# Differential-attention heads with two buffer sets and the order q, k, v; at the SwiGLU's seam half a row scaling on ScalarE and one token sum on GpSimd

## The chip, the cores and the metric

The kernel runs on one core of a Trainium2 chip. The metric is the device time of one execution in microseconds (us). Times of several runs are given as their median; a profile is one further execution, with a time of its own.

## What is computed

One layer of a streaming encoder block over 512 tokens of width 1024, with 16 meta tokens put ahead of them (528 rows in all), everything in float32:

```
xn   = rmsnorm(h)
proj = xn @ w_in                      # stick-breaking q|k|v, differential q|k|v; 8 heads each
o_sb = stick_breaking_attention(sq, sk, sv)          # strictly causal, no softmax
p    = softmax(dq @ dk + alibi bias, masked)         # two maps per head, c = 0, 1
o_df = rmsnorm((p[0] - lam * p[1]) @ dv) * (1 - lam_init)
gates  = sigmoid(xn @ w_gate + b_gate)
merged = gates[0] * (o_sb @ w_br_sb) + gates[1] * (o_df @ w_br_df)
h = h + merged @ w_out
h = h + (silu(hn @ w_ffn_gate) * (hn @ w_ffn_up)) @ w_ffn_down      # hn = rmsnorm(h)
y = rmsnorm(h), meta rows dropped
```

A stick-breaking head has 128 columns. A differential head has two maps of 64 columns for q and k, and 128 columns for v.

## The kernel before, in words

**Arithmetic.** Every float32 matrix product is made of three products of a rounded high part and a remainder: high times high, high times low, low times high (`mm3`, L224; its three matmuls stand at L227, L228 and L229 wherever it is called). So every operand has to be split: a cast on ScalarE (L75) and a subtraction on VectorE (L76).

**Weights.** They are read from HBM once, in 512 KB pieces, in the order of the list `stream` (L86 to L117). A piece lands in one of three staging tiles `wst` (issued from SyncE's queue, L144), is split into `wh` and `wl` (four buffers each), and is then used. `weights(key)` (L215) also has the next pieces split: three ahead before the first differential piece, two ahead after it (L221).

**Stages by time.** 0 to 40 us: norm and transposes of x. Then eight stick-breaking heads, up to about 260 us; eight differential heads, up to about 510; the gates and the merge (540 to 593); `merged @ w_out` (to 640); the SwiGLU's gate and up products; its down product; the final norm.

**One head.** While head h computes its scores and maps, TensorE is also given units of other work: the projections of head h+1 (two units each for q, k and v), the transposition of head h+1's v (`turn`), and two units of a branch projection `y` of earlier heads. The generator `df_head` (L622) yields numbers, and the loop at L948 runs so many units at each yield. In the differential heads the units stand in the order v, q, k (L618), then the first y unit, `turn`, the second y unit. So between the scores of the token tiles 0, 1, 2 and 3 lie v, v and the first half of q; after the last scores come the rest of q and the two halves of k; then `t1` (transposes of the attention weights), a y unit, `t2` (the rest of these transposes), `turn` and the second y unit, and then `av` (attention weights times v).

**Program order and issue order.** The head loop is not in a hand-written order: the framework's scheduler orders the instructions of each engine by priority among those that it holds ready, so that an engine can be given a later unit where an earlier one would wait. [...] The framework also puts in every wait, and it hands out the buffers of a tag in a ring: a new tile waits until the tile that had the buffer has been read for the last time.

**q and k of a differential head.** Each map c has a tile `dq`, 128 x 512: rows of one half hold the high part, rows of the other half the remainder; and a tile `dk`, 128 x 2 x 528. ScalarE and VectorE write one half of `dk`'s partitions (L611, L612), and a DMA from GpSimd's queue copies this half to the other partitions (L615). There is one buffer of each, so that the next head's q can only be written when the present head's scores have been made. The scores are made at L632 and L633.

**PSUM.** Eight banks: `z`, two tiles of two banks each, for scores, for the transposes of the attention weights (L493, L507, L510, in the function `attn_out`, L482), and for `av`; and `mm`, four tiles of one bank (`mm_tile`, `tr_tile`), for projections, y units, `turn` and the heads' norm. In `attn_out`, `turn_first` makes the transposes of blocks 0 and 1 into the two banks of one `z` tile, and `turn_rest` makes block 2 and the small blocks into another. Each block is read by ScalarE (L495) and then by VectorE (L496).

**y.** A y tile of 128 x 512 is copied out of PSUM by ScalarE (L725) into a buffer, from which a DMA on GpSimd's queue writes it to DRAM, or adds it there (L727, L729). The buffers are, in turn, one of two `ys` and one of two `sg0` tiles; for the last two y pieces four tiles named w0 to w3.

**The tag y_sb in the pool xtp.** One buffer of 16 KB a partition. The tile `tA` (token sums for the stick-breaking heads, L272) has it first, and then `hres` (L997), into which the residual input x is loaded in four DMAs of 512 KB (L999, GpSimd's queue). `hres` is first read at L1031.

**The tag y_df in opool.** One buffer too: `xs` (the input), then `tB` (more token sums for the stick-breaking heads), then `hn` (L1054).

**The seam.** Between `merged @ w_out` and the SwiGLU stand the row norm (`normed`, L1057: the row's reciprocal root r, then `hn = hres * r` on VectorE, 128 x 1024, once for each of four token tiles), the transposes (`turned`, L1061), and sums and differences of blocks of the transposed tokens (`block_sums`, L1080), from which the SwiGLU's seven-product form takes its operands t1 to t4. TensorE's first products with t2 wait on L1089, VectorE's remainder of t2.

Of the kernel before, what the change touches and what calls it, by code (L numbers as in the profile page):

```python
# [9 lines left out]
F32 = mybir.dt.float32  # L10
F32R = mybir.dt.float32r
# [5 lines left out]
P = 128  # L17
# [23 lines left out]
def block_kernel(ctx: ExitStack, tc: tile.TileContext, x, meta, norm_mix_g, w_in, w_gate, b_gate,  # L41
# [50 lines left out]
    for h in range(NH):  # L92
        for i in (2, 0, 1):
            cols(("df", h, i), w_in, (3 + i) * D + h * P)
        if h < 3:
            rows(("y_sb", h + 5), w_br_sb, (h + 1) % 2 * 512, (h + 5) // 2 * 2)
        else:
            rows(("y_df", h - 3), w_br_df, (h + 1) % 2 * 512, (h - 3) // 2 * 2)
# [116 lines left out]
    def weights(key):  # L215
        at = at_of[key]
        if at < START:
            return loaded[key]
        if at >= first_ffn:
            return fpools["down"](key)  # L220
        prepare(prep_at[key] + (READY if at < at_of["df", 0, 2] else 2))  # L221
        return loaded[key]
# [46 lines left out]
    ydram = ctx.enter_context(tc.tile_pool(name="ydram", bufs=1, space=bass.MemoryType.DRAM))  # L269
    y_count = [0]  # L270

# [209 lines left out]

    def attn_out(blocks, d, lo_rows):  # L482

# [14 lines left out]
        def turn_first():  # L498
            z = z_tile()
            turn(0, z[:, 0])  # L500
            turn(1, z[:, 1])

        def turn_rest():
            z = z_tile()
            turn(2, z[:, 0])
            pt = z[:, 1]
            nc.tensor.transpose(pt[:, 384:512], blocks(3, 3 * P, 4 * P), ident)  # L507
# [42 lines left out]
    def sb_head(h, d, o_h, o_l):  # L550
# [31 lines left out]
        base = ((0, 0), (0, 144), (0, 416), (1, 0))  # L582
        t1, t2, av = attn_out(lambda t, k0, k1: res[base[t][0]][:, base[t][1] + k0:base[t][1] + k1], d, 96)
        yield 4 if h + 1 < SEVEN else 5
# [9 lines left out]
    def df_units(h):  # L594
        d = {}
        hs = (slice(0, 64), slice(64, 128))
        q = [ap_.tile([P, SEQ], F32R, tag=("qh", "ql")[c], name=f"dq{c}") for c in range(2)]
        k = [ap_.tile([P, 2, L], F32R, tag=("kh", "kl")[c], name=f"dk{c}") for c in range(2)]
        d["q"], d["k"] = q, k
# [17 lines left out]
        kv, turn = kv_all("df", h, k_evac, d)  # L617
        return d, kv[2:4] + halves(("df", h, 0), xT, QT, q_evac) + kv[0:2], turn  # L618

    late = []  # L620

    def df_head(h, d, o_h, o_l):  # L622
# [55 lines left out]
        maps(3)  # L678
        t1, t2, av = attn_out(lambda t, k0, k1: prs[t][:, 0, k0:k1], d, 64)
        yield 3 if h < NH - 1 else 2  # L680
        t1()
        yield 1
        t2()
        yield 2
        ps = av()
# [23 lines left out]
    def y_units(name, i, o):  # L709

        def unit(fs):
            wh, wl = weights((name, i))
            for f in fs:
                ps = mm_tile()
                cs = slice(f % 4 * P, (f % 4 + 1) * P)
                mm3(ps, [(wh[:, k, cs], wl[:, k, cs], o[0][:, k], o[1][:, k]) for k in range(2)])

                if name == "y_df" and i > 5:
                    ys = ap_.tile([P, SEQ], F32, tag=f"w{y_count[0] % 4}", name="ys")
                elif y_count[0] % 2:  # L720
# [200 lines left out]
    for br in range(2):  # L921
        name, head = (("y_sb", sb_head), ("y_df", df_head))[br]
        if br:
            nc.gpsimd.memset(a_s, 0.0)
        for h in range(NH):
            if (br, h) == (0, 0):
# [130 lines left out]
    def normed(t):  # L1057
        r = rstd(ssq[t][:, 1:2], more=ssq[t][:, 0:1])()
        nc.vector.tensor_scalar(hn[:, t], hres[:, t], r, None, op0=ALU.mult)

# [19 lines left out]
    def block_sums():  # L1080
# [3 lines left out]
        split(*tsum["t1"], b11)  # L1084
        nc.vector.tensor_tensor(b12, b22, b12, op=sub)
        nc.vector.tensor_tensor(b22, b11, b22, op=add)
        th, tl = tsum["t2"]
        nc.scalar.activation(th, b22, AF.Copy, scale=-1.0)
        nc.vector.scalar_tensor_tensor(tl, b22, -1.0, th.bitcast(F32), op0=ALU.mult, op1=sub)  # L1089
        nc.vector.tensor_tensor(b21, b22, b21, op=sub)  # L1090
        for n, v in (("t3", b12), ("t4", b21)):
# [199 lines left out]
```

## Time and profile before

| what | value |
|---|---|
| time, three runs | 997.58, 999.05, 1001.49 us; median 999.05 us |
| the profiled execution: its own time | 1000.49 us |
| the profiled execution: span from the first to the last instruction | 998.6 us |
| mean granted TensorE clock | 0.993 |
| TensorE matmuls, busy | 970.5 us (97%) |
| VectorE, busy | 687.9 us (69%) |
| ScalarE, busy | 572.2 us (57%) |
| GpSimd, busy | 158.2 us (16%) |
| moved by DMA | 114.12 MB, mean 114 GB/s |

All times below count from the start of the span. PE is TensorE's matmul, PEld its weight load, DVE VectorE, ACT ScalarE, POOL GpSimd, SP SyncE; an L and a number name a line of the kernel. A row of the timeline has the start, the length, the engine, the line, the operation, the tiles written and read, the shapes and the count; in square brackets how long the engine had been idle and what ended this. A row of the list of waits says who waited for whom: the total, the number of times and the longest. A row of a table by stretches has, for each engine, its busy time and in brackets the number of its instructions; then the granted TensorE clock, the busy share of the DMA engines and the GB/s. [...]

### The profile page before, as it was taken

How to read it: one execution, taken by the hardware profiler on the slowest of the kernel's cores; microseconds unless marked ns; L12 is line 12 of the kernel's file. 1: busy time of each engine (PE TensorE's matmuls, PEld its weight loads, DVE VectorE, ACT ScalarE, POOL GpSimd, SP SyncE). 2: the span in 40 equal slices, each digit the busy share in tenths (PEclk: the TensorE clock that was granted, in tenths of full speed). 3: DMA queues.
4: the chain of work that ended last, by engine and by line, in shares of the span. 5: the costliest groups of instructions: out<-in, count | busy, mean ns of one | idle time of the engine just before them, and what ended most of it. 6: DMA issues, size and time to landing. Idle time of an engine off the chain costs nothing.

```text
span 998.6 us, 16211 instructions
## 1 busy us (share of the span) xinstructions
PE 970.5 (97%) x6213; PEld 870.4 (87%) x6213; DVE 687.9 (69%) x1244; ACT 572.2 (57%) x1091; POOL 158.2 (16%) x216
## 2 busy tenths in 40 slices
PE   7999999989999999999999999989999999999996
PEld 5998888879888998889878888879999999988885
DVE  8998678764567777678632633798888888754544
ACT  5676766665566666666772533575555555643533
POOL 4010112121232222322314530000000000000103
PEclk9999999998999999999999999999999999999999
DMA  7312444465563444643838732223343434332212
GB/s 214 86 43 65 127 131 96 97 190 127 127 142 105 93 129 128 148 109 92 161 84 209 223 117 85 85 78 114 94 118 94 119 90 122 100 112 99 92 43 85
DMA packets 140241, 114.12 MB, mean 114 GB/s; under 512 B 4962, under 2 KB 115715, under 8 KB 140163
## 3 DMA queue, kind: packets, MB, share of 16 engines
q1 hardware_dynamic: 129810, 89.29, 29.7%
q0 software_dynamic: 10192, 23.73, 11.9%
q8 instruction: 49, 0.80, 0.3%
q14 instruction: 30, 0.24, 0.1%
q10 hardware_dynamic: 160, 0.07, 0.0%
HBM read 89.87 MB, written 18.87 MB: 109 GB/s over the span
## 4 chain that ended last, share of the span: by engine, by line
PE 78%; DVE 8%; ACT 6%; DMA 5%; issue 2%; POOL 1%; SPq 0%; DVEq 0%; POOLq 0%; ACTq 0%
PE mm L229 18%; PE mm L227 18%; PE mm L228 18%; PE z L227 6%; PE z L229 6%; PE z L228 6%; DMA dk<-dk 3%; PE z L493 1%; ACT wh L75 1%; PE z L632 1%; DVE wl L76 1%; PE z L633 1%; DMA wst<-in_w_in_dram 1%; DVE s L578 1%; DMA xs<-in_x_dram 1%
## 5 line engine op out<-in xcount | busy, mean ns | idle before, releaser
L76 DVE TENSOR_TENSOR wl<-wst,wh 128x1024 fp32r<-128x1024 f32 (+1 forms) x150 | 170.0, 1137 | 118.9 <-ACT wh L75 118.7
L228 PE MATMUL mm<-xT_l,wh 128*128 128x264 f32 (+2 forms) x656 | 213.7, 326 | 2.2 <-DVE xT_l L828 2.2
L227 PE MATMUL mm<-xT_h,wh 128*128 128x264 f32 (+2 forms) x656 | 214.6, 327 | 0.6 <-ACT xT_h L827 0.6
L229 PE MATMUL mm<-xT_h,wl 128*128 128x264 f32 (+2 forms) x656 | 213.5, 325 | 0.0
L75 ACT CAST wh<-wst 128x1024 fp32r<-128x1024 f32 (+1 forms) x150 | 145.8, 972 | 98.9 <-PE mm L228 40.4
L228 PEld LDWEIGHTS mm<-xT_l,wh 128*128 128x128 f32 x656 | 124.2, 189 | 11.6 <-DVE xT_l L828 2.4
L227 PEld LDWEIGHTS mm<-xT_h,wh 128*128 128x128 f32 x656 | 124.4, 190 | 10.3 <-ACT xT_h L827 1.1
L229 PEld LDWEIGHTS mm<-xT_h,wl 128*128 128x128 f32 x656 | 124.1, 189 | 9.8
L228 PE MATMUL mm<-hT_l,wh 128*128 128x256 f32 x284 | 80.5, 284 | 0.7 <-DVE hT_l L1074 0.7
L227 PE MATMUL mm<-hT_h,wh 128*128 128x256 f32 x284 | 80.2, 284 | 0.6 <-DVE sg L1169 0.6
L229 PE MATMUL mm<-hT_h,wl 128*128 128x256 f32 x284 | 80.1, 283 | 0.0
L660 ACT ACTIVATE pr<-pr,nm 128x144 f32<-128x144 f32 (+3 forms) x64 | 36.3, 568 | 40.4 <-DVE nm L658 40.4
L228 PEld LDWEIGHTS mm<-hT_l,wh 128*128 128x128 f32 x284 | 53.7, 189 | 1.2 <-DVE hT_l L1074 1.1
L227 PEld LDWEIGHTS mm<-hT_h,wh 128*128 128x128 f32 x284 | 53.4, 189 | 1.1 <-DVE sg L1169 0.7
L229 PEld LDWEIGHTS mm<-hT_h,wl 128*128 128x128 f32 x284 | 53.6, 189 | 0.0
L227 PE MATMUL mm<-o_h,wh 128*128 128x512 f32 x128 | 52.3, 410 | 0.3 <-ACT o_h L703 0.3
L229 PE MATMUL mm<-o_h,wl 128*128 128x512 f32 x128 | 51.6, 404 | 0.0
L228 PE MATMUL mm<-o_l,wh 128*128 128x512 f32 x128 | 50.0, 392 | 0.0
L227 PE MATMUL mm<-t_h,wh 128*128 128x256 f32 x168 | 47.4, 282 | 1.3 <-ACT wh L75 1.0
L228 PE MATMUL mm<-t_l,wh 128*128 128x256 f32 x168 | 47.3, 281 | 1.1 <-DVE t_l L1089 1.1
L475 POOL COPY v_s<-vT 128x16 f32<-128x16 f32 x64 | 17.8, 307 | 190.6 <-ACT vT L480 82.3
L229 PE MATMUL mm<-t_h,wl 128*128 128x256 f32 x168 | 47.3, 281 | 0.0
(314 smaller groups left out, 2508.0 us busy)
## 6 DMA issues: line engine op xcount, KB each, us to landing
wst<-in_w_in_dram SPq DMA_DIRECT2D x40, 512.0 KB, 4.1
wst<-in_w_ffn_gate_dram SPq DMA_DIRECT2D x22, 512.0 KB, 3.7
wst<-in_w_ffn_down_dram SPq DMA_DIRECT2D x22, 512.0 KB, 3.5
wsu<-in_w_ffn_up_dram SPq DMA_DIRECT2D x21, 512.0 KB, 3.8
wst<-in_w_gate_dram SPq DMA_DIRECT2D x16, 512.0 KB, 4.6
y_df<-ys POOLq DMA_DIRECT2D x20, 256.0 KB, 6.2
dk<-dk POOLq DMA_DIRECT2D x16, 264.0 KB, 5.8
wst<-in_w_br_sb_dram SPq DMA_DIRECT2D x8, 512.0 KB, 4.9
```

Of the source, the lines that this page charges most:

```text
L75: (hi_copy or nc.scalar.copy)(hi, src)
L76: (lo_eng or nc.vector).tensor_tensor(lo, src, hi.bitcast(F32), op=ALU.subtract)
L227: nc.tensor.matmul(ps, lhsT=ah, rhs=bh, start=(start and i == 0), stop=False, skip_group_check=skip)
L228: nc.tensor.matmul(ps, lhsT=ah, rhs=bl, start=False, stop=False, skip_group_check=skip)
L229: nc.tensor.matmul(ps, lhsT=al, rhs=bh, start=False, stop=(stop and i == n - 1), skip_group_check=skip)
L475: nc.gpsimd.tensor_copy(v_s[:, 32 * t:32 * t + NM], vT[:, (t + 1) * P:(t + 1) * P + NM])
L493: nc.tensor.transpose(pt[:, (t - j) * P:(t - j + 1) * P], blocks(t, j * P, (j + 1) * P), ident)
L578: nc.vector.tensor_tensor_scan(f, f, f, 0.0, op0=ALU.add, op1=ALU.bypass)
L632: nc.tensor.matmul(o, lhsT=q[c][:, qs], rhs=k[c][:, 0, k0:k1], start=True, stop=False)
L633: nc.tensor.matmul(o, lhsT=q[c][:, qs], rhs=k[c][:, 1, k0:k1], start=False, stop=True)
L660: nc.scalar.activation(pr[:, c], pr[:, c], AF.Exp, bias=nm[:, c:c + 1], accum_out=ls[:, t, c:c + 1])
```

## The change

1. The pieces of a differential head are streamed and projected in the order q, k, v instead of v, q, k; the look-ahead of weights changes at the first differential piece as before, which is now q.
2. Differential heads with an odd number have their q and k in a second set of buffers: one tile `dqk` in opool's tag `y_df`. Heads with an even number keep the old buffers.
3. In differential heads the transposes of the attention weights go to four `mm` tiles of one bank each instead of two `z` tiles. Stick-breaking heads keep `z`.
4. After `t2` one unit is run ahead of `av` instead of two.
5. From the start of the differential branch on, the y copies go in turn to the eight slots of one new tile `y_out`. It takes the tag `y_sb` in xtp, between `tA` and `hres`.
6. At the seam, `hn` is made in two halves, columns 0 to 511 on VectorE and 512 to 1023 on ScalarE.
7. In `block_sums` the difference `b12 = b22 - b12` (128 x 1024) moves from VectorE to GpSimd, and the sum behind it is written to `b11` instead of `b22`, so that it needn't wait for that difference.

```diff
     for h in range(NH):
-        for i in (2, 0, 1):
+        for i in range(3):
             cols(("df", h, i), w_in, (3 + i) * D + h * P)
...
-        prepare(prep_at[key] + (READY if at < at_of["df", 0, 2] else 2))
+        prepare(prep_at[key] + (READY if at < at_of["df", 0, 0] else 2))
...
-    y_count = [0]
+    y_count, y_out = [0], []
...
-    def attn_out(blocks, d, lo_rows):
+    def attn_out(blocks, d, lo_rows, banks):
...
         def turn_first():
-            z = z_tile()
-            turn(0, z[:, 0])
-            turn(1, z[:, 1])
+            for j, pt in enumerate(banks()):
+                turn(j, pt)
 
         def turn_rest():
-            z = z_tile()
-            turn(2, z[:, 0])
-            pt = z[:, 1]
+            p2, pt = banks()
+            turn(2, p2)
...
     # sb_head
-        t1, t2, av = attn_out(lambda t, k0, k1: ..., d, 96)
+        t1, t2, av = attn_out(lambda t, k0, k1: ..., d, 96,
+                              lambda: (lambda z: (z[:, 0], z[:, 1]))(z_tile()))
...
     def df_units(h):
-        q = [ap_.tile([P, SEQ], F32R, tag=("qh", "ql")[c], name=f"dq{c}") for c in range(2)]
-        k = [ap_.tile([P, 2, L], F32R, tag=("kh", "kl")[c], name=f"dk{c}") for c in range(2)]
+        if h % 2:
+            both = opool.tile([P, 4 * L + 2 * SEQ], F32R, tag="y_df", name="dqk", bufs=1)
+            q = [both[:, 4 * L + c * SEQ:4 * L + (c + 1) * SEQ] for c in range(2)]
+            k = [both[:, 2 * c * L:2 * (c + 1) * L].rearrange("p (a l) -> p a l", a=2) for c in range(2)]
+        else:
+            q = [ap_.tile([P, SEQ], F32R, tag=("qh", "ql")[c], name=f"dq{c}") for c in range(2)]
+            k = [ap_.tile([P, 2, L], F32R, tag=("kh", "kl")[c], name=f"dk{c}") for c in range(2)]
...
-        return d, kv[2:4] + halves(("df", h, 0), xT, QT, q_evac) + kv[0:2], turn
+        return d, halves(("df", h, 0), xT, QT, q_evac) + kv, turn
...
     # df_head
-        t1, t2, av = attn_out(lambda t, k0, k1: prs[t][:, 0, k0:k1], d, 64)
+        t1, t2, av = attn_out(lambda t, k0, k1: prs[t][:, 0, k0:k1], d, 64, lambda: (tr_tile(), tr_tile()))
         yield 3 if h < NH - 1 else 2
         t1()
         yield 1
         t2()
-        yield 2
+        yield 1
         ps = av()
...
     # y_units
-                if name == "y_df" and i > 5:
-                    ys = ap_.tile([P, SEQ], F32, tag=f"w{y_count[0] % 4}", name="ys")
+                if y_out:
+                    ys = y_out[0][:, y_count[0] % KT]
                 elif y_count[0] % 2:
...
         if br:
             nc.gpsimd.memset(a_s, 0.0)
+            y_out.append(xtp.tile([P, KT, SEQ], F32, tag="y_sb", name="y_out"))
...
     def normed(t):
-        nc.vector.tensor_scalar(hn[:, t], hres[:, t], r, None, op0=ALU.mult)
+        nc.vector.tensor_scalar(hn[:, t, 0:512], hres[:, t, 0:512], r, None, op0=ALU.mult)
+        nc.scalar.activation(hn[:, t, 512:D], hres[:, t, 512:D], AF.Copy, scale=r)
...
     # block_sums
-        nc.vector.tensor_tensor(b12, b22, b12, op=sub)
-        nc.vector.tensor_tensor(b22, b11, b22, op=add)
+        nc.gpsimd.tensor_tensor(b12, b22, b12, op=sub)
+        nc.vector.tensor_tensor(b11, b11, b22, op=add)
         th, tl = tsum["t2"]
-        nc.scalar.activation(th, b22, AF.Copy, scale=-1.0)
-        nc.vector.scalar_tensor_tensor(tl, b22, -1.0, th.bitcast(F32), op0=ALU.mult, op1=sub)
-        nc.vector.tensor_tensor(b21, b22, b21, op=sub)
+        nc.scalar.activation(th, b11, AF.Copy, scale=-1.0)
+        nc.vector.scalar_tensor_tensor(tl, b11, -1.0, th.bitcast(F32), op0=ALU.mult, op1=sub)
+        nc.vector.tensor_tensor(b21, b11, b21, op=sub)
```

More of the change, by code (lines that the diff above doesn't have):

```diff
@@ L582, in sb_head @@
         base = ((0, 0), (0, 144), (0, 416), (1, 0))
-        t1, t2, av = attn_out(lambda t, k0, k1: res[base[t][0]][:, base[t][1] + k0:base[t][1] + k1], d, 96)
+        t1, t2, av = attn_out(lambda t, k0, k1: res[base[t][0]][:, base[t][1] + k0:base[t][1] + k1], d, 96,
+                              lambda: (lambda z: (z[:, 0], z[:, 1]))(z_tile()))
         yield 4 if h + 1 < SEVEN else 5
```

## The prediction

> **What bounds the kernel now.** I read the page, then the list of waits of TensorE, then a table by stretches, and at each stretch where TensorE was short of work the timelines of the engines.
>
> ```profile
> span 998.6 us, 16211 instructions
> PE 970.5 (97%) x6213; PEld 870.4 (87%) x6213; DVE 687.9 (69%) x1244; ACT 572.2 (57%) x1091; POOL 158.2 (16%) x216
> ```
>
> TensorE is the bound, nearly everywhere. So an edit can gain only where TensorE waits or runs slowly, and no more than that: about 28 us of 998.6 over the whole span, of which the first 40 us (the start) are not touched. The waits of TensorE over the whole span, the ones that the change can reach:
>
> ```profile
> PE z L507 <- DVE a_l L496: 2.7, 1, 2.7
> PE z L632 <- DMA dk<-dk: 2.2, 6, 0.6
> PE tr L476 <- POOL v_s L475: 1.3, 2, 1.0
> PE mm L228 <- DVE t_l L1089: 1.1, 1, 1.1
> ```
>
> And one of the same list asked for 240 to 540 us alone, the differential heads:
>
> ```profile
> PE z L493 <- DVE a_l L496: 1.4, 4, 0.4
> ```
>
> The longest wait of all, 2.7 us, lies in a stick-breaking head that the change seems not to touch. Here are the stretches around it (PE, PEld, DVE, ACT, POOL busy; then the granted clock, the DMA share and GB/s):
>
> ```profile
> 211.00:214.00 3.00, 3.00 (x15) 2.47 (x14) 3.00 (x5) 1.75 (x3) 0.00 (x0) 1.00 1.01 407
> 223.00:226.00 3.00, 1.38 (x7) 1.00 (x8) 2.70 (x4) 1.86 (x7) 1.97 (x4) 0.67 0.32 92
> 226.00:230.00 4.00, 4.00 (x16) 3.71 (x15) 0.39 (x2) 0.65 (x3) 0.87 (x1) 0.50 0.93 186
> 230.00:235.00 5.00, 5.00 (x28) 4.33 (x26) 1.56 (x3) 3.43 (x7) 0.85 (x1) 0.91 0.59 118
> ```
>
> The engines' timelines, and from the chain of waits the row of the DMA:
>
> ```profile
> 208.75 2.18 POOL L999 DMA_DIRECT2D hres<-in_x_dram  x4 [2.34 <-PE mm L229]
> 213.30 7.11 DMA wst<-in_w_in_dram
> 220.49 1.05 ACT L75 CAST wh<-wst 128x1024 fp32r<-128x1024 f32 x1 [3.29 <-DMA wst<-in_w_in_dram]
> 222.18 1.04 ACT L75 CAST wh<-wst 128x1024 fp32r<-128x1024 f32 x1 [0.35 <-DMA wst<-in_w_in_dram]
> 223.13 0.74 ACT L495 CAST a_h<-z 128x384 fp32r<-128x384 f32 x2
> 223.68 0.88 DVE L496 TENSOR_TENSOR a_l<-z,a_h 128x384 fp32r<-128x384 f32 x2
> 224.62 0.47 PE L507 MATMUL z<-ident,s 128*128 128x128 f32 x1 [2.70 <-DVE a_l L496]
> ```
>
> And the DMA issues with size and time to landing:
>
> ```profile
> wst<-in_w_in_dram SPq DMA_DIRECT2D x40, 512.0 KB, 4.1
> hres<-in_x_dram POOLq DMA_DIRECT2D x4, 512.0 KB, 5.1
> ```
>
> The four loads of `hres`, 2 MB, are issued at 208.75, as soon as a TensorE product has read `tA` for the last time. They fill the DMA engines (407 GB/s). A weight piece issued in the middle of them, at 213.30, takes 7.11 us instead of the median 4.1. ScalarE's queue stands at that piece's cast for 3.29 us and then at the next one's; behind them stand the casts `a_h` that TensorE needs; TensorE waits 2.70 us, and then runs at half clock to about 231.
>
> **Part by part: y_out and hres.** The change says nothing of `hres`, but it puts `y_out` between `tA` and `hres` in the one buffer of their tag. So the four loads can't start before the last y copy has left `y_out`:
>
> ```profile
> 531.62 0.87 POOL L729 DMA_DIRECT2D y_df<-ys  x1 [0.77 <-ACT ys L725]
> 540.00:610.00 70.00, 70.00 (x311) 57.96 (x310) 30.10 (x29) 26.34 (x35) 26.91 (x16) 1.00 0.53 166
> L1031 DVE TENSOR_TENSOR hres<-hres,z x9: 407/681/690, 614.0 to 991.9; 128x512 f32<-128x512 f32 x8, 128x256 f32<-128x256 f32 x1
> ```
>
> That is after 531.62 plus a landing, about 538, and `hres` is first read at 614.0: some 75 us for 5.1 us loads. There TensorE never waits (70.00 busy of 70) and the DMA share is 0.53; gate weights and y read-backs lie in the way, and if their slack were gone it could cost what it costs now. I take 0.
>
> What goes at 213: with the median landing the piece is there at 217.4 and not at 220.4, 3.0 us sooner, and the row of casts behind it moves with it, which is more than the 2.70 us wait. Gain: the wait, 2.70, and the clock: 3 us x 0.33 + 4 us x 0.50 + 5 us x 0.09 = 3.4 us of lost full speed, of which some 0.3 lies under the wait. Together **5.8 us**; the bounds are 0 (the piece is late anyway) and 5.8. [...]
>
> The y copies' own waits for a free buffer hold up ScalarE, not TensorE, in the gate stretch: 0.
>
> **Order q, k, v and two buffer sets.** Rows of the first differential head, as an example of the wait for k's second half:
>
> ```profile
> 264.08 0.28 PE L633 MATMUL z<-dk,dq 128*128 128x256 f32 x1
> 264.67 0.39 PE L632 MATMUL z<-dk,dq 128*128 128x256 f32 x1 [0.32 <-DMA dk<-dk]
> 264.90 0.28 PE L633 MATMUL z<-dk,dq 128*128 128x256 f32 x1
> 265.01 0.29 PE L632 MATMUL z<-dk,dq 128*128 128x272 f32 x1
> ```
>
> The `dk` copies' landing times, and from the chain a matmul of 512 columns:
>
> ```profile
> DMA to landing us min/median/max: 5.0/5.8/6.9
> 242.06 0.23 PE mm L227
> ```
>
> From start to start the disturbed pair takes 0.59 and the undisturbed one 0.11, so a listed wait of 0.32 costs 0.48: 0.16 us of restart on top. The `dk` copy (5.8 us) is issued near the end of a head now. With v behind k, two v units are put between: 24 matmuls a unit at half of 0.23 us, 2.8 us each, 5.5 for both, then the transposes, two y units of 12 x 0.23 = 2.8 us, and `av`. That is over 11 us against 5.8, so the wait is gone with room to spare. Gain: 2.2 + 6 x 0.16 = 3.2 us. The second buffer set is what allows q first, as no score of the present head then stands in the way of writing q; it costs no instruction. Nothing is late next in its place, except v: its `turn` comes sooner after it. Heads of which v is the last piece are in the trace already: the stick-breaking ones, with TensorE's 1.3 us for `v_s` (L476, at most 1.0) in the first list. I put 1.3 us against the gain; bounds 0 and 8 x 1.0.
>
> **Transposes in mm banks.** The wait for `a_l` inside a head:
>
> ```profile
> 376.58 0.60 PE L493 MATMUL z<-ident,pr 128*128 128x128 f32 x4
> 379.84 0.67 DVE L496 TENSOR_TENSOR a_l<-z,a_h 128x512 fp32r<-128x512 f32 x1
> 380.56 0.55 PE L493 MATMUL z<-ident,pr 128*128 128x128 f32 x3 [0.41 <-DVE a_l L496]
> ```
>
> Block 1's three transposes start when VectorE has read block 0, though they write the other bank of the `z` tile: the tile is one thing to the waits. With a tile for each bank this wait has no ground. Gain: 1.4 + 4 x 0.16 = 2.0 us. Against it: 16 tiles a head instead of 12 go through the four `mm` banks (a rival, below). The unit that moves behind `av` leaves only `turn` as cover for `av`'s operands; but the scheduler fills such a place with the next ready unit, as it did above, where block 1 was passed by a y unit. Cost 0. The heads together: 3.2 + 2.0 - 1.3 = **3.9 us**.
>
> **The seam.**
>
> ```profile
> 544.33 1.28 POOL L991 TENSOR_TENSOR sg<-sg,y_sb 128x512 f32<-128x512 f32 x1
> 544.39 1.76 DVE L992 TENSOR_TENSOR sg<-sg 128x512 f32<-128x512 f32 x1 [8.57 <-POOL sg L991]
> 551.74 0.69 DVE L992 TENSOR_TENSOR sg<-sg 128x512 f32<-128x512 f32 x1 [1.18 <-POOL sg L991]
> 657.33 1.22 DVE L1085 TENSOR_TENSOR bf<-bf 128x1024 f32<-128x1024 f32 x1
> 645.14 0.75 DVE L1059 TENSOR_SCALAR hn<-hres,rs 128x1024 f32<-128x1024 f32 x1
> 994.15 0.72 ACT outs L1247
> ```
>
> `hn`: half a row on ScalarE takes 0.72 (the same scaling in the final norm), as long as the whole row on VectorE, 0.75: 0. The sum on GpSimd: VectorE loses a 1.22 us instruction ahead of t2, and TensorE's 1.1 us wait for t2 could go, 1.3 us with its restart. But the sum, twice as wide as L991's, takes about 2 x 1.28 = 2.6 us, and a VectorE operation on two SBUF tiles that runs into such a GpSimd operation takes 1.76 instead of 0.69. [...] Bounds -1.3 and +1.3; I take 0.
>
> **Sum.** 5.8 + 3.9 + 0 = 9.7 us. Against the profiled execution's own 1000.49 that is 990.8; the median of the runs shown, 999.05, lies 1.4 lower, and the forecast is for a median: 999.05 - 9.7 = 989.4, say **989.4 us**.
>
> **Rivals.**
> - *The late weight stays* (another transfer, or the order of ScalarE's queue, makes it late without `hres`). For it: the DMA share is 0.93 also at 226 to 230, when `hres` is through. Against: no other transfer is slowed so with TensorE idle. 999.05 - 3.9 = 995.2.
> - *The heads gain nothing*: new waits for `mm` banks or v eat the 5.2. 999.05 - 5.8 = 993.3.
> [...]
> - *`hres` collides in its new place*, with the gate weights: 5.8 given back, 995.2.
> - *The ring of mm banks becomes the bound; slower.* A block's bank is held from 376.58 to 379.84 + 0.67, 3.9 us. The unit moved behind `av` takes the banks of `t2`'s blocks. If these are held as long, TensorE has only `turn` (0.6) and half the unit (1.4) to fill 3.9: it stands 1.9 us in each of eight heads, 15 us, and the time is 999.05 - 9.7 + 15 = 1004. It decides from 9.7 / 8 = 1.2 us a head. Against it: the blocks of `t2` are small, and `av` can't start before they are read anyway.
>
> **How the numbers follow.** Forecast 0.62; late weight 0.13; heads 0.10; clock 0.04; collision 0.05; ring 0.06. No change is told from one only beyond 0.5%, 5 us, that is outside 994.1 to 1004.0. The forecast and the clock count as faster (0.66), of the heads case, which lies near the edge, 0.06 of 0.10; late weight and collision are mostly within; the ring is slower, with a little for what I don't see. Faster 0.72, same 0.21, slower 0.07. Range: everything gained, 5.8 + 5.2 + 1.3 = 12.3, gives 986.8, and the runs lie up to 1.5 under their median: 985. Above, the late weight's and the collision's 995.2 with some scatter: 996. The ring is left out.
>
> **What would show it.** `hres` issued after 530 and not at 208.75; the pieces of that head landing in about 4 us; no clock below 1.00 between 220 and 235; no wait of L632 for `dk`; L493 without waits for `a_l`, block 1 straight behind block 0; L1085 on GpSimd near 2.6 us with a longer VectorE operation beside it. The prediction is wrong if the clock still falls there, or if the eight differential heads together don't get some 4 us shorter.

## The result, and the profile after

The changed kernel takes 989.02 us (median of 4 runs, 987.64 to 990.32), beside 998.86 for the kernel before on the same chip (4 runs, 997.58 to 1001.49): a ratio of 0.9906 with an interval of 0.9887 to 0.9924. The changed kernel run again in another set of runs gave 989.13 beside 997.68, 0.9910 (0.9892 to 0.9927). It is faster by 9.8 us; 9.7 were forecast.

The page of the changed kernel: the span, and the busy times.

```profile
span 988.6 us, 16198 instructions
PE 965.0 (98%) x6213; PEld 870.6 (88%) x6213; DVE 675.2 (68%) x1243; ACT 575.3 (58%) x1095; POOL 168.7 (17%) x217
```

TensorE is the bound as before, with the same 6213 matmuls. Its own waits over the whole span (who waited for whom: total, times, longest):

```profile
PE mm L227 <- DVE sg L1175: 2.7, 1, 2.7
PE z L493 <- DVE a_l L496: 2.2, 2, 1.4
...
PE tr L476 <- POOL v_s L475: 1.3, 2, 1.0
...
PE z L505 <- DVE a_l L496: 0.2, 1, 0.2
```

The 2.7 us wait at 224 is gone, with the waits for `dk`, and v has not taken their place: `v_s` has the 1.3 us that it had. But a new wait of the old one's length has come: 2.7 us for L1175, in the SwiGLU. The two waits that L493 still has for `a_l` lie in stick-breaking heads, which keep `z`: 0.8 us at 61, as before, and 1.4 us at 250, in the eighth head, which is new.

The waits alone don't say what a stage gained, nor do the lengths of the matmuls, which overlap (in the kernel before the 128x512 matmul at 220.40 takes 0.39 us, and the next one starts at 220.63). For that I took the start of one matmul at each border of a stage (the first score matmul of a head; the first matmul of the product) and subtracted:

| stage | before, us | after, us | difference |
|---|---|---|---|
| start to the first head | 38.18 | 39.70 | +1.52 |
| seventh to eighth stick-breaking head (the late weight) | 33.67 | 28.38 | -5.29 |
| eighth stick-breaking to first differential head | 30.30 | 30.83 | +0.53 |
| first to eighth differential head, seven distances | 216.45 | 209.78 | -6.67 |
| eighth differential head to the end of the gates | 112.82 | 111.86 | -0.96 |
| `merged @ w_out` and norm | 45.53 | 44.99 | -0.54 |
| seam and SwiGLU, to the down product | 227.94 | 229.22 | +1.28 |
| all others | 293.73 | 293.79 | +0.06 |
| span | 998.62 | 988.55 | -10.07 |

The first row is scatter between executions: the same stage takes 38.04 to 40.31 in the profiles of this study, also of kernels that are alike there (the changed kernel again: 38.04). The row of the seam scatters too: it takes 227.65 to 229.36 us in the five profiles of kernels whose seam is that of before. The 0.53 us of the eighth stick-breaking head come with the order q, k, v: that stage takes 30.82 us with the order alone and 30.04 in the changed kernel with the old order.

**The late weight.** First GpSimd's timeline of the changed kernel, with the four `hres` loads, in two pairs, and the sum that is now on GpSimd:

```profile
533.02 1.13 POOL L1004 DMA_DIRECT2D hres<-in_x_dram  x2 [5.25 <-DMA y_df<-y_out]
535.41 1.13 POOL L1004 DMA_DIRECT2D hres<-in_x_dram  x2
...
644.20 2.45 POOL L1091 TENSOR_TENSOR bf<-bf 128x1024 f32<-128x1024 f32 x1 [58.19 <-ACT bf L1083]
```

The loads went out at 533 instead of 208.75, held by the last y copies. The chain of waits has a weight piece, ScalarE's timeline the cast that waits for it, and the table by stretches the head that it used to stop (busy time of PE, PEld, DVE, ACT, POOL; granted clock, DMA share, GB/s):

```profile
215.98 5.24 DMA wst<-in_w_in_dram
221.31 1.05 ACT L75 CAST wh<-wst 128x1024 fp32r<-128x1024 f32 x1 [1.22 <-DMA wst<-in_w_in_dram]
```

```profile
223.00:226.00 3.00, 2.77 (x17) 2.01 (x16) 2.18 (x5) 1.60 (x6) 1.10 (x2) 1.00 0.87 201
226.00:230.00 4.00, 4.00 (x26) 3.51 (x25) 1.16 (x2) 2.01 (x6) 0.99 (x2) 1.00 1.07 241
...
540.00:610.00 70.00, 70.00 (x311) 57.97 (x309) 27.61 (x32) 26.40 (x39) 17.95 (x10) 1.00 0.46 146
```

Two weight pieces are issued here, 1.1 us apart, in both kernels (at 213.30 and 214.41 in the kernel before). For the first, which took 7.11 us, nobody waits any more. The row is that of the second: 5.24 us, where the trace of before has 7.67 for it. There are 17 and 26 matmuls where there were 7 and 16; and the clock is at 1.00 where it was 0.67 and 0.50. In its new place `hres` costs nothing: 70.00 busy of 70.

**The differential heads.** Three score and `av` rows of TensorE's timeline before, and the same rows after:

```profile
355.73 0.60 PE L523 MATMUL z<-a_s,vf 128*128 128x256 f32 x2
355.97 0.47 PE L632 MATMUL z<-dk,dq 128*128 128x256 f32 x1
...
386.91 0.47 PE L632 MATMUL z<-dk,dq 128*128 128x256 f32 x1
```

```profile
347.14 0.60 PE L521 MATMUL z<-a_s,vf 128*128 128x256 f32 x2
347.39 0.58 PE L227 MATMUL mm<-o_h,wh 128*128 128x512 f32 x1
...
350.34 0.28 PE L637 MATMUL z<-dqk 128*128 128x256 f32 x1
...
380.36 0.28 PE L637 MATMUL z<-dk,dq 128*128 128x256 f32 x1
```

From first score to first score a head took 30.94 us and now takes 30.02. One thing more is to be seen here: before, the next head's scores stood straight behind the last `av` matmul, and the first of them took 0.47; now a y unit stands between (347.39 to 350.34), and it takes 0.28.

**The seam.** VectorE's timeline of the changed kernel. L174 prepares a weight of the SwiGLU; the first row is the same operation, undisturbed:

```profile
637.39 0.68 DVE L174 TENSOR_TENSOR s<-s,wst 128x512 f32<-128x512 f32 x1
...
644.46 2.73 DVE L174 TENSOR_TENSOR s<-s,wst 128x512 f32<-128x512 f32 x1
647.12 0.68 DVE L181 TENSOR_TENSOR wsu<-wst,wsu 128x512 f32<-128x512 f32 x1
647.72 0.41 DVE L1175 TENSOR_TENSOR sg<-mm,q 128x256 f32<-128x256 f32 x1
```

The table by stretches at the same place:

```profile
645.00:648.00 3.00, 0.46 (x2) 0.19 (x1) 3.00 (x3) 2.87 (x4) 1.65 (x1) 1.00 0.00 0
648.00:651.00 3.00, 2.81 (x15) 2.81 (x16) 3.00 (x5) 0.32 (x2) 0.00 (x0) 0.63 0.02 5
```

While GpSimd adds (644.20 to 646.65), L174 takes 2.73 us; it ends at 647.19, 0.54 after GpSimd. L1175, for which TensorE waits 2.7 us, comes behind it on VectorE, at 647.72; TensorE has 2 matmuls in 3 us, and a granted clock of 0.63 in the next 3.

### The profile page after: what moved, and what is told of

Read it like the earlier page. It is cut to its first block, busy times and chain, and to the rows that moved or that the text cites. A ratio compares the mean times of both kernels' runs of the same rounds, so it can differ in the third digit from the quotient of the medians.

```text
span 988.6 us, 16198 instructions
## 1 busy us (share of the span) xinstructions
PE 965.0 (98%) x6213; PEld 870.6 (88%) x6213; DVE 675.2 (68%) x1243; ACT 575.3 (58%) x1095; POOL 168.7 (17%) x217
## 4 chain that ended last, share of the span: by engine, by line
PE 85%; DVE 7%; ACT 5%; DMA 1%; issue 1%; POOL 0%; SPq 0%; DVEq 0%; ACTq 0%; POOLq 0%
PE mm L229 20%; PE mm L227 20%; PE mm L228 20%; PE z L227 6%; PE z L229 6%; PE z L228 6%; PE z L638 1%; PE z L637 1%; ACT wh L75 1%; DVE s L576 1%; PE tr L493 1%; PE tr L469 1%; PE z L493 1%; DVE wl L76 1%; PE z L521 1%
## 5 line engine op out<-in xcount | busy, mean ns | idle before, releaser
L228 PEld LDWEIGHTS mm<-xT_l,wh 128*128 128x128 f32 x656 | 123.5, 188 | 11.2 <-DVE xT_l L832 2.0
L641 DVE CUSTOM_DVE_ANT_0 pr<-z,bias 128x144 f32<-128x144 f32 (+3 forms) x64 | 31.0, 502 | 34.9 <-PE z L638 34.8
L475 POOL COPY v_s<-vT 128x16 f32<-128x16 f32 x64 | 26.3, 440 | 162.4 <-DVE vT L405 78.1
L1261 POOL TENSOR_TENSOR outs<-hres,gF 128x512 f32<-128x512 f32 x4 | 5.1, 1287 | 262.1 <-DVE hres L1036 261.2
```

The costliest lines, as they stand in the source:

```text
L228: nc.tensor.matmul(ps, lhsT=ah, rhs=bl, start=False, stop=False, skip_group_check=skip)
L475: nc.gpsimd.tensor_copy(v_s[:, 32 * t:32 * t + NM], vT[:, (t + 1) * P:(t + 1) * P + NM])
L641: nc.vector.tensor_tensor_reduce(po, zz, bb, scale=1.0, scalar=-3.0e38, op0=ALU.add, op1=ALU.max, accum_out=mx[:, t, c:c + 1])
```

## The experiments

My theory was that of the prediction: the late weight and the heads bring the gain, the seam nothing. It was put to test one part at a time, first added to the kernel before (e1 to e4), then taken out of the changed kernel (e5 to e7, e10 to e12). Ratios are to the kernel before on the same chip. The kernel before has medians of 998.9, 999.9 and 997.7 us in the three sets of runs (e1 to e4, e5 to e8, e9 to e12), so times from different sets compare to a microsecond or two only.

### y_out alone

The kernel before with part 5 only:

```diff
-                if name == "y_df" and i > 5:
-                    ys = ap_.tile([P, SEQ], F32, tag=f"w{y_count[0] % 4}", name="ys")
+                if y_out:
+                    ys = y_out[0][:, y_count[0] % KT]
...
+            y_out.append(xtp.tile([P, KT, SEQ], F32, tag="y_sb", name="y_out"))
```

> The kernel before with part 5 alone (y copies into y_out, hres behind it). Theory (hres collides with a weight piece at 213 us): hres issued after 530 us, no TensorE wait of 2.7 us and no half clock between 220 and 235 us, time 5.8 us under the kernel before, about 993.1. Rival (the gain of the change is made in the heads and at the seam, the late weight stays): the wait and the half clock stay, time within 1 us of before.

996.03 us, ratio 0.9969 (0.9957 to 0.9981). GpSimd's timeline and one stretch:

```profile
540.77 1.11 POOL L1000 DMA_DIRECT2D hres<-in_x_dram  x2 [5.75 <-DMA y_df<-y_out]
```

```profile
223.00:226.00 3.00, 3.00 (x23) 2.64 (x22) 1.29 (x3) 1.15 (x5) 1.63 (x2) 1.00 0.99 205
```

The stage goes from 33.67 to 27.94 us, so the mechanism is shown: the place of one tile in a ring of buffers moves four loads by 332 us (208.75 to 540.77) and takes the stall away. But the median falls by 2.9 us, not by 5.8. The stall in the profile of before was an unusually dear one: over the undisturbed 28.2 us, the stage costs 5.5 more there, but 3.0 and 3.4 in the next two experiments that keep it.

### hres late, by another tile

The kernel before with an unused tile between `tA` and `hres`, written once (one column) after the last gate:

```diff
     att.close()
+    held = xtp.tile([P, KT, SEQ], F32, tag="y_sb", name="held")
+    nc.scalar.copy(held[:, 0, 0:1], sg1[1][:, 0:1])
```

> The kernel before, its y copies and their buffers as they were; only hres is held back: an unused tile stands between tA and hres in their buffer and is written once, one element wide, after the last gate's sigmoid. Theory (only the time of hres counts): the same as part 5 alone, 5.8 us under before, about 993.1, half clock gone. Rival (the eight slots of the y copies count, as ScalarE no longer waits for a free one): no more than 1 us under before, about 998, although hres is late.

1000.85 us, ratio 1.0015 (1.0000 to 1.0029). The stall at 222 goes as well (the stage takes 28.22 us), but nothing is gained. The time by itself would have spoken for the rival, the eight slots; the trace shows what takes the gain back. The instructions of `hres`; GpSimd's first sum in the merge, which reads y back; TensorE's row; and two stretches:

```profile
L1001 POOL DMA_DIRECT2D hres<-in_x_dram x4: 858/878/1126, 519.1 to 531.8; - x4
```

```profile
543.02 1.28 POOL L993 TENSOR_TENSOR sg<-sg,y_sb 128x512 f32<-128x512 f32 x1 [10.41 <-DMA y_sb<-y_sb]
```

```profile
549.81 0.50 PE L227 MATMUL mm<-xT_h,wh 128*128 128x512 f32 x1 [2.27 <-ACT sg L736]
```

```profile
535.00:540.00 5.00, 5.00 (x24) 4.14 (x23) 0.00 (x0) 0.00 (x0) 0.00 (x0) 1.00 1.07 334
...
550.00:555.00 5.00, 5.00 (x16) 3.95 (x16) 3.04 (x3) 1.49 (x4) 3.60 (x2) 0.66 0.70 200
```

Here the loads go out between the last y copies, at 519.1 to 531.8 on the same queue, and at 535 to 540 they still move, with the last y pieces and two weight pieces, 334 GB/s (154 at that time in the kernel before). These two weight pieces take 16.9 and 11.2 us to land; in the kernel before they take 7.2 and 7.4. VectorE, ScalarE and GpSimd stand still for these 5 us; the first sum of the merge comes at 543.02 (541.84 before), and TensorE runs dry at 547.5 for 2.27 us, waiting for a sigmoid on ScalarE, and then has 0.66 of the clock. Ahead of this sigmoid ScalarE now also has a weight's cast of 1.04 us, which stood behind it before; how much of the wait is the cast's was not separated. The stage up to the end of the gates takes 116.78 us instead of 112.82. So the rival "`hres` collides in its new place" holds for this kernel, at 4.0 us. In the changed kernel the loads wait for the last y copy to have left `y_out` (the 5.25 us in the row at 533.02), and y is read back from 507 on, not from 539; TensorE does not wait there. Which of the two keeps the loads out of the way was not tried.

### The order alone

The kernel before with parts 1 and 2 (order q, k, v; two sets):

```diff
-        for i in (2, 0, 1):
+        for i in range(3):
...
+        if h % 2:
+            both = opool.tile([P, 4 * L + 2 * SEQ], F32R, tag="y_df", name="dqk", bufs=1)
...
-        return d, kv[2:4] + halves(("df", h, 0), xT, QT, q_evac) + kv[0:2], turn
+        return d, halves(("df", h, 0), xT, QT, q_evac) + kv, turn
```

> The kernel before with parts 1 and 2 alone (order q, k, v; second set of q and k for odd heads); transposes stay in z, hres stays at 208 us. Theory: no wait of the scores for dk, 3.2 us saved less up to 1.3 us for v: 2 to 3 us under before, about 996.3; half clock at 220 to 235 us stays. Rival (dk was only the last of several waits): the scores or the transposes wait for something else as long, time within 1 us of before.

996.87 us, ratio 0.9984 (0.9969 to 1.0000): near the 996.3 of the theory, but not by its way. All waits for `dk` are gone, and yet a head takes 30.84 us instead of 30.94. Over all seven distances 1.6 us are gained, mostly in the first and the last; the eighth stick-breaking head loses 0.5 and the stage behind the heads 0.7, so that the rival, `dk` as the last of several waits, is nearer the truth. In the place of the `dk` wait stand small ones: for `a_l` and, behind `av`, the slow first score (0.47 again). The long waits of this profile, and the stretches around the late weight, which this kernel keeps:

```profile
PE z L507 <- DVE a_l L496: 3.0, 1, 3.0
PE z L493 <- DVE a_l L496: 2.8, 3, 1.3
```

```profile
223.00:226.00 3.00, 1.10 (x8) 0.86 (x9) 2.97 (x4) 2.09 (x7) 2.21 (x4) 1.00 0.18 51
226.00:229.00 3.00, 3.00 (x21) 2.78 (x20) 0.81 (x3) 1.66 (x5) 0.87 (x1) 1.00 1.10 225
```

The stall is a little longer than before, 3.0 us, and the clock doesn't fall at all: the stage costs 3.0 us, the wait and no more.

### The banks alone

The kernel before with part 3 (transposes of a differential head in four `mm` tiles):

```diff
-        t1, t2, av = attn_out(lambda t, k0, k1: prs[t][:, 0, k0:k1], d, 64)
+        t1, t2, av = attn_out(lambda t, k0, k1: prs[t][:, 0, k0:k1], d, 64, lambda: (tr_tile(), tr_tile()))
```

> The kernel before with part 3 alone (transposes of differential heads into four mm banks). Theory: no wait of L493 for a_l in the differential heads, 2.0 us under before, about 996.9; waits for dk stay. Rival (four mm banks are too few for 16 tiles a head): TensorE waits at y units or turn for a bank, time at or above before by up to 15 us.

1003.28 us, ratio 1.0033 (1.0018 to 1.0048): slower. A head takes 31.58 us, 0.64 more. Of the list of waits of TensorE:

```profile
PE mm L227 <- ACT sg L724: 2.9, 7, 0.4
PE z L505 <- DVE a_l L496: 1.9, 1, 1.9
PE mm L227 <- DVE dk L611: 1.4, 6, 0.2
```

These are waits for an `mm` bank, once in nearly every head: for ScalarE's y copy and for the eviction of k. The prediction's rival of the ring is true of this part alone, at half of the price from which it was to decide.

### The changed kernel without y_out

```diff
-                if y_out:
-                    ys = y_out[0][:, y_count[0] % KT]
+                if name == "y_df" and i > 5:
+                    ys = ap_.tile([P, SEQ], F32, tag=f"w{y_count[0] % 4}", name="ys")
...
-            y_out.append(xtp.tile([P, KT, SEQ], F32, tag="y_sb", name="y_out"))
```

> The changed kernel without part 5: y copies into the old buffers, hres again directly behind tA. Theory (hres collides at 213 us and the heads don't need y_out): the wait of about 2.8 us in the seventh stick-breaking head is back, with none, one or two stretches of 3.4 us at half clock behind it, so that the profile's stretch from the seventh to the eighth head is 3 to 5.5 us longer than the changed kernel's 28.38; heads stay at 30.03 us; median 2.8 to 5 us above the changed kernel, about 993. Rival (the heads' gain hangs on the eight y slots): the heads go back toward 30.8 us as well, median about 998.

991.44 us, ratio 0.9913 (0.9891 to 0.9936); the changed kernel had 0.9906 and 0.9910, so the two can't be told apart by their intervals. The heads keep their 30.03 us: part 5 has nothing to do with them. GpSimd's timeline and TensorE's wait:

```profile
209.77 2.18 POOL L1003 DMA_DIRECT2D hres<-in_x_dram  x4 [2.34 <-PE mm L229]
```

```profile
PE z L505 <- DVE a_l L496: 1.0, 1, 1.0
```

The four loads are back in their old place: 8.83 us after the seventh head's first score, as in every kernel that has them there (it reads 209.77 and not 208.75 because the heads start 0.9 us later in this execution). Yet the stall is 1.0 us, not the 2.8 of the theory, with the granted clock at 1.00 from 220 to 230, and the stage takes 29.15. What differs is how long the second weight piece takes, which is issued 14.49 us after that score in all five kernels:

| kernel (one profile each) | second piece to landing, us | TensorE's wait, us |
|---|---|---|
| order alone | 8.00 | 3.04 |
| before | 7.67 | 2.70 |
| banks alone | 6.88 | 1.87 |
| changed, without y_out | 6.01 | 1.00 |
| changed (no loads beside it) | 5.24 | 0.2 |

The wait is the landing time less 4.96 to 5.01 us in the first four. So the collision is the cause of the wait in each of them, and its size varies from profile to profile; why the piece takes 6.0 us in one and 8.0 in another stays open.

### The changed kernel with two units ahead of av

Part 4 undone:

```diff
         t2()
-        yield 1
+        yield 2
         ps = av()
```

> The changed kernel without part 4: two units ahead of av again. Theory (scores directly behind av wait for the z bank that av's copy holds, 0.19 + 0.13 + 0.10 us a head in the traces of before and of the order alone): heads about 30.4 instead of 30.03 us, median 2.5 to 3.5 us above the changed kernel, about 992. Rival (the scheduler fills either place with what is ready): no difference, 989.

992.89 us, ratio 0.9926 (0.9905 to 0.9947). A head takes 30.59 us: the moved unit, put at 0 in the prediction, is worth 0.56 us in this one and 3.1 over the seven distances. TensorE's timeline, the same place as above, with one weight load:

```profile
349.35 0.60 PE L521 MATMUL z<-a_s,vf 128*128 128x256 f32 x2
349.60 0.47 PE L637 MATMUL z<-dqk 128*128 128x256 f32 x1
349.90 0.28 PE L638 MATMUL z<-dqk 128*128 128x256 f32 x1
...
350.68 0.19 PEld L637 LDWEIGHTS z<-dqk 128*128 128x128 f32 x1 [0.35 <-ACT of L695]
...
380.19 0.47 PE L637 MATMUL z<-dk,dq 128*128 128x256 f32 x1
```

The next head's scores come straight behind `av` again. The second score starts 0.30 after the first instead of 0.11, and at 350.68 the weight load of the next token tile's scores waits 0.35 for ScalarE's copy of `av` (L695). By the starts of the matmuls this place loses 0.50 us in all; the head's norm (L702, whose weight load waits for GpSimd) and a y unit lose 0.1 each. The changed kernel in turn loses 0.19 at the y unit behind `av`, which accounts for the 0.56 but for a few hundredths.

### The changed kernel with the sum on VectorE

Only the GpSimd move of part 7 undone:

```diff
-        nc.gpsimd.tensor_tensor(b12, b22, b12, op=sub)
+        nc.vector.tensor_tensor(b12, b22, b12, op=sub)
```

> The changed kernel without the move of part 7: the difference b12 back on VectorE, the sum behind it still in b11. Theory (the GpSimd sum of 2.45 us shuts VectorE out, whose 0.68 us sum at L174 takes 2.73, and TensorE's wait of 2.70 us behind it): L174 back at 0.7 us, that wait gone, some of it given back as a wait for t2 of about 1 us; median 1 to 3 us under the changed kernel, about 987. Rival (the seam is bound by ScalarE's queue, casts and table loads): the waits move to other instructions, within 0.7 us of the changed kernel.

986.30 us, ratio 0.9861 (0.9837 to 0.9884), the fastest of all. VectorE's timeline:

```profile
644.36 1.22 DVE L1091 TENSOR_TENSOR bf<-bf 128x1024 f32<-128x1024 f32 x1
645.50 0.42 DVE L1175 TENSOR_TENSOR sg<-mm,q 128x256 f32<-128x256 f32 x1
...
646.96 0.69 DVE L174 TENSOR_TENSOR s<-s,wst 128x512 f32<-128x512 f32 x1
```

The sum costs VectorE 1.22 us, L174 takes 0.69 again, L1175 comes at 645.50 and not at 647.72, and the wait for it shrinks to 0.5 us. No half clock follows: the granted clock is 1.00 from 645 to 651. The stage goes from 229.22 to 226.36, 2.86 us, much as the medians say (989.0 to 986.3); by the ratios, which allow for the different sets, it is 4.5 to 4.9.

### The last stick-breaking head's transposes in mm banks

On top of the last kernel, against the 0.53 us that the eighth stick-breaking head lost:

```diff
-                              lambda: (lambda z: (z[:, 0], z[:, 1]))(z_tile()))
+                              lambda: (tr_tile(), tr_tile()) if h == NH - 1 else (lambda z: (z[:, 0], z[:, 1]))(z_tile()))
```

> As the run with the difference back on VectorE, and the last stick-breaking head's transposes also in four mm banks, where the changed kernel has a wait of 1.36 us for a_l. Theory (the two banks of a z tile count as one thing): that wait goes, 1 to 1.5 us under the run without this edit, about 985.7. Rival (four mm banks are too few there, as v is the last piece and the first y units follow): a wait for a bank in its place, no gain.

986.69 us, ratio 0.9865 (0.9843 to 0.9886): no change. The list of waits of TensorE:

```profile
PE mm L227 <- ACT vT L480: 1.3, 1, 1.3
PE z L493 <- DVE a_l L496: 0.9, 1, 0.9
```

The wait of 1.4 us for `a_l` becomes one of 1.3 for an `mm` bank that ScalarE reads.

### The changed kernel again

Run to have it beside the next three on one chip.

> The changed kernel itself, beside the next three on the same chip: about 989.0. [...]

989.13 us. The wait of 2.7 us for L1175 and the slow stretch behind it are there again (granted clock 0.88 from 645 to 648, 0.55 from 648 to 651): the same picture as in its first profile. The last section sets it beside the other gaps.

### The changed kernel with z banks, and with the old order

Part 3 undone in the one, parts 1 and 2 in the other (the hunks of the two "alone" experiments above, the other way round):

```diff
-        t1, t2, av = attn_out(..., d, 64, lambda: (tr_tile(), tr_tile()))
+        t1, t2, av = attn_out(..., d, 64, lambda: (lambda z: (z[:, 0], z[:, 1]))(z_tile()))
```

> The changed kernel without part 3: transposes of differential heads in z tiles again, with order q, k, v, two sets and one unit ahead of av. Theory (each part of the heads is worth something beside the others): block 1 waits for block 0's a_l, heads about 30.3 to 30.4 instead of 30.03 us, median 2 to 3 us above the changed kernel, about 991.5. Rival (the banks were a loss alone, 0.67 us a head, and order with the moved unit make the gain): heads at 30.0 or below, median 989 or below.

```diff
-        for i in range(3):
+        for i in (2, 0, 1):
...
-        return d, halves(("df", h, 0), xT, QT, q_evac) + kv, turn
+        return d, kv[2:4] + halves(("df", h, 0), xT, QT, q_evac) + kv[0:2], turn
```

> The changed kernel without parts 1 and 2: order v, q, k and one set of q and k, but transposes in mm banks and one unit ahead of av. Theory (k last, its bank held by four reads in turn, stands in the way of the ring of mm banks, and the scores wait for dk): heads 30.4 to 31.0 us, median 3 to 7 us above the changed kernel, 992 to 996. Rival (the moved unit covers dk and the ring as well): heads about 30.05 us, median 989.

994.07 us (0.9958, 0.9943 to 0.9972) and 995.59 us (0.9972, 0.9958 to 0.9986), so 4.9 and 6.5 above the changed kernel on the same chip. A head takes 30.59 and 30.98. With `z` banks, TensorE's weight loads wait for VectorE's `a_l` again, once in each differential head (list of waits, 260 to 505 us); with the old order, the wait for an `mm` bank is back:

```profile
PEld z L493 <- DVE a_l L496: 3.7, 8, 0.5
```

```profile
PE mm L227 <- ACT y_out L723: 2.9, 7, 0.4
```

"Order" is parts 1 and 2, which were not tried apart, "banks" part 3, "moved unit" part 4. The distance of the first scores from the fourth to the fifth differential head, and the sum of all seven distances:

| parts in the kernel | us a head | seven, us |
|---|---|---|
| none (before) | 30.94 | 216.45 |
| order | 30.84 | 214.82 |
| banks | 31.58 | 220.61 |
| order and moved unit | 30.59 | 213.60 |
| banks and moved unit | 30.98 | 217.00 |
| order and banks | 30.59 | 212.90 |
| all three | 30.03 | 209.78 |

The moved unit alone was not run.

### The sum on VectorE and hn in one piece

Both parts of the seam undone, except that the sum behind b12 still goes to b11:

```diff
-        nc.gpsimd.tensor_tensor(b12, b22, b12, op=sub)
+        nc.vector.tensor_tensor(b12, b22, b12, op=sub)
...
-        nc.vector.tensor_scalar(hn[:, t, 0:512], hres[:, t, 0:512], r, None, op0=ALU.mult)
-        nc.scalar.activation(hn[:, t, 512:D], hres[:, t, 512:D], AF.Copy, scale=r)
+        nc.vector.tensor_scalar(hn[:, t], hres[:, t], r, None, op0=ALU.mult)
```

> The changed kernel with both parts of the seam undone (hn wholly on VectorE, b12 on VectorE; only the sum in b11 stays). Theory (half a row on ScalarE takes as long as the whole on VectorE): as with the difference alone back on VectorE, about 986.3, within 0.7 us of it. Rival (the split shortens the path from the row's root to the transposes, the stretch from the output product to the SwiGLU is 0.54 us shorter with it): 0.5 to 1 us longer than that, about 987.

988.48 us, ratio 0.9902 (0.9885 to 0.9920). Beside the kernel with only the sum on VectorE (986.30, on another chip) it is 2.2 us slower, and in the profiles 0.54 (`merged @ w_out` and norm, 45.53 against 44.99) and 1.36 (seam, 227.72 against 226.36), 1.9 together. The first of these is the same in all profiles: 44.99 to 45.01 us in the eight with the split, 45.52 or 45.53 in the six without. So the rival is right, and its gain larger than it said. What the split had removed, in its list of waits of TensorE:

```profile
PE mm L228 <- DVE t_l L1094: 1.0, 1, 1.0
PE mm L228 <- DVE hT_l L1079: 0.7, 2, 0.4
PE z L227 <- ACT t_h L75: 0.4, 1, 0.4
```

## Why the prediction was right

The total was met, by terms that were off in both directions; that they cancel to 0.1 us is luck.

- **The late weight, 5.8: mechanism right, size wrong.** `hres` was the cause, and moving it took the stall away. The term measured 2.9 us in the medians (alone; interval 1.9 to 4.3), and 5.3 in the profile. The step that failed is "the wait, 2.70, and the clock ... 3.4": it priced one execution. In that one the clock was halved for 6.83 us (224.04 to 230.87); the wait with the order alone was 3.0 us and cost no clock. The wait itself ranges from 1.0 to 3.0 us with the landing of one piece, and that is the second of the two: the prediction worked from the first. No run shows the case that has 0.04 for the clock, the half clock without the gap: where the gap went, with y_out alone, with `hres` late and in the changed kernel, the granted clock was 1.00 from 223 to 230.
- **Heads, 3.2 + 2.0 - 1.3 = 3.9: too small.** The stages give 6.67 + 0.96 - 0.53 = 7.1 us. Without the moved unit the same three stages give 3.4 us, so the sum for parts 1 to 3 is nearly right, but not by its terms. The `dk` waits went as predicted, and v cost nothing, where 1.3 had been set against the gain. But the terms don't add: over the seven distances the order alone gives 1.6 us, the banks alone lose 4.2, the two together give 3.6, and all three 6.7. As long as one of them is missing, another wait stands where the first has gone (the table of heads).
- **"Cost 0" for the unit moved behind `av`: wrong by 0.56 us a head, as a gain.** It is the other half of the heads, 3.7 us of the 7.1. The prediction asked what the unit had covered in its old place; it did not ask what it covers in the new one, the scores straight behind `av`.
- **The ring of `mm` banks:** not the bound in the changed kernel, but it is with the banks alone or with the old order. The order of the units keeps it away, with the unit behind `av` moved or not; the prediction's reason, the small blocks of `t2`, was not tried.
- **The seam, 0 with bounds of 1.3: two errors that hid each other.** The split of `hn`, put at 0 because each half is as long as the whole, gains about 2 us: by the waits that went, the whole row on VectorE stood in front of operations that TensorE waits for. That is read from the lists; no run takes it apart. The GpSimd sum loses 2.9, outside the bound. The bound of -1.3, VectorE's 2.6 lost against 1.22 saved, was an estimate that no run shows; in its place the profile shows a delay of 2.2 at L1175 (645.50 to 647.72: 2.73 of L174 and 0.6 of L181 in front of it, against 1.22 and less), a wait of 2.7 for 0.5, and 3.4 us of half clock behind it, 1.7 of lost time; some of this comes back later, since 2.86 is what the stage lost. The sum written to `b11` stays in all the runs and was not tried apart.
- **`hres` in its new place and the y copies, 0:** right in the changed kernel; one variant shows 4.0 us for the former.

What of the late weight's gain is left in the changed kernel is not settled: without y_out it is 2.4 us slower by the medians but 0.3 to 0.7 by the ratios, in different sets of runs, and 0.8 in this stage of the profiles.

The best version that came out of it is the changed kernel with the sum on VectorE, 986.30 us.

## What to carry to other kernels

A wait that goes uncovers the one behind it: test edits to one stage together and each taken away, since alone they may show next to nothing (0.10 us a head) or the wrong sign (0.64). Where a transfer is issued can be set by a buffer that nobody thinks of; look at what frees the tile it writes, and at what is on the DMA engines at that time. Before an elementwise operation goes to GpSimd, look at which VectorE operations run beside it (here one of 0.68 us took 2.73 beside a sum of 2.45), and at who waits behind those.

## What the runs showed of the hardware

**The clock after a gap.** In the profiles of the kernel before and of the changed kernel the granted clock falls to one half for 3.41 us (at 15.83 in the one, at 24.13 and 648.77 in the other) or 6.83 us (at 224.04 in the kernel before) at a time, the very end of the span aside. But the same gap does not always bring it. TensorE's 2.70 us at 222 in the kernel before was followed by the 6.83 us, the 3.0 us with the order alone by none (1.00 from 223 to 229), the 1.9 us with the banks alone by about 3.4, the 1.0 us without y_out by none (1.00 from 220 to 230). The 2.7 us at the seam was followed by 3.41 in the changed kernel and about 3.4 in its second profile (0.88 and 0.55, above), and by more without y_out (0.98 from 645 to 648, 0.50 from 648 to 651) and with two units ahead of `av`: the pages of these two have 0.8 for the clock of that fortieth of the span, those of the changed kernel, of z banks and of the old order 0.9 or more. The rows of the banks-alone kernel, with its 1.9 us wait above:

```profile
223.00:226.00 3.00, 1.64 (x8) 1.29 (x9) 2.83 (x6) 1.96 (x8) 1.65 (x4) 0.80 0.41 115
226.00:229.00 3.00, 3.00 (x16) 2.81 (x15) 0.00 (x0) 0.35 (x2) 0.87 (x1) 0.63 1.07 202
```

What decides between these was not shown. For a price, the dip behind a 2 to 3 us gap was between 0 (order alone) and 3.4 us of lost time (half of the 6.83), and one profile shows one draw of it.

**GpSimd beside VectorE.** Beside a 2.45 us sum on GpSimd, a VectorE operation that reads two SBUF tiles and takes 0.68 us at 637.39 (L174) took 2.73 us, and ended 0.54 after GpSimd; in the five other profiles with this sum on GpSimd it took 2.73 or 2.74, and in those with the sum on VectorE 0.68 or 0.69. In the kernel before, L992 beside GpSimd's 1.28 us sum at 544.33 took 1.76 us, where it takes 0.69 at 551.74, and ended 0.54 after GpSimd too.
